# Hybrid decoder layer on one core: key weights in the values' region, the second norm's sums in PSUM, chunk 0's weight sums ahead of the FFN

## The chip, the core and the metric

The kernel runs on one core of a Trainium2 chip. Engines, as the profile names them: PE (matmul, with PEld for its weight loads), DVE (vector), ACT (scalar, activation), POOL (general), SP (issues most of the DMAs). Each has its own queue and runs it in order; semaphores tie them together. SBUF is the working memory (128 partitions), PSUM holds matmul outputs in eight banks of 128 x 512 fp32. The metric is device time in microseconds. The kernel before takes 1085.76 us, the median of three runs (1084.98 to 1085.92).

## The reference

One decoder layer over 1024 tokens of width 1024, fp32:

```python
h = rms_norm(x, mix_norm)
z = h @ w_in          # gq, gk, gv, gr, glr, sq, sk, sv
# gated linear attention (4 heads), sliding-window attention with sinks (8 query, 2 kv heads)
x = x + concat([o_gla, o_swa]) @ w_out
h2 = rms_norm(x, ffn_norm)
u = causal_dwconv(h2 @ w_up, conv_w, conv_b)      # 2 x 2816 columns, 3 taps
a, bval = split(u, 2)
return x + (silu(a) * bval) @ w_down
```

## The kernel before

**Numbers and tiles.** Every fp32 operand of a large matmul is split into a high part (a cast to fp32r) and a low part (source minus high part), and each product takes three passes: high x high, high x low, low x high (`PASSES`). `split` (L85) does this: ACT casts the high part, POOL (or the engine given) subtracts. Tokens lie in 8 tiles of 128. `big` holds the split, transposed activations of all tiles, first of the first norm, then of the attention output, then of the second norm.

**Stages.** One matmul stage follows another, each with a unit per token tile: query (`unit_q`), key with gate columns (`unit_k`, 272 columns), values (`unit_v`), gated q and k (`unit_g`), output gate (`unit_r`), and output projection in two halves of 512 columns (`unit_o`). The small matmuls of the two attentions run between them. The weights of a stage come as 4 raw loads (two row blocks each) into a ring of three raw tiles, and become 8 split pieces (`load_piece` L265, `piece` L256). The pieces lie in nine slots of 4 KB, w0 to w8, dealt out by the tuple `SLOTS` (L72): query 0 to 7, key 8 and 0 to 6, values 7, 8, 0 to 5, and so on. Key pieces fill only 272 of a slot's 512 columns.

**Key and value stage.** `kvl_post` (L325) takes a key tile out of PSUM: squares on ACT, sum on DVE, the power -1/2 on POOL (`rms_scale` L151, the power at L155), the scaled keys kn on DVE (L332). `kvl_tr` (L338) transposes kn on PE. The first norm's buffers (`px`) give way to the values' result `vg` (16 KB, `open_vg`), which the value units write.

**Second norm.** After the second half of a token tile's output projection, `norm2_stat` (L178) squares the row on ACT and takes the power on POOL; `norm2_tr` (L185) scales the row on DVE (L188, two halves) and transposes it on PE into two PSUM banks. Tiles 0 to 3 are split straight into `big`. For tiles 4 to 7, `norm2_sums` (L201) also forms the sums that the FFN's fast products need: b12 is copied by ACT from PSUM; T1 = b12 - b11 on POOL (on DVE for tile 7, `T1_DVE`); T3 = b22 - b12, T2 = b22 - T1, T4 = b21 - T2 on DVE, into four SBUF tiles; each is split into `big` or `ex`, the low parts partly on POOL, partly on DVE. The temporaries lie in the pool `pn`, whose space the FFN's pool `ff` takes over at `open_ff`.

**FFN.** The up projection is cut into 22 chunks of 128 columns of a and of b. A chunk is a 2 x 2 block product over halves of the width and halves of the tokens, done as seven products (`PROD`, L724) of 12 matmuls of 128x512: P1 (A11, B11), P2 (A12, B21), P3 (S4, B22), P4 (A22, T4), P5 (S1, T1), P6 (S2, T2), P7 (S3, T3). The weight sums are S1 = A21 + A22, S3 = A11 - A21, S2 = S1 - A11, S4 = A12 - S2, formed by POOL in place in the raw tiles; `up_operand` (L691) forms and splits them. Chunk 0 runs P1, P2, P3, P5, P6, P7, P4. Its P1 and P2 and chunk 1's come first (the list `LOW`), for they need token tiles 0 to 3 alone. From then on two chunks' products and the down projection (also by seven products, `down_pair`) interleave to the end.

**Order.** Each step is entered by hand with a due time (`at`, in units of a token tile; `at_us`, in us from the FFN's start TU), and the steps are emitted in order of that time. The framework then lays out each engine's order by a simulated timeline (`schedule_with_timeline_sim=True`), with the emitted order as priority: what is ready in the simulation may go ahead of what is not. A tile in a reused slot or in a reopened region waits for the last user of what lay there. PSUM banks are dealt alternately from two pools of four (`bank` L55); at the FFN's start all eight become fixed banks fb0 to fb3 and gb0 to gb3.

The due times that matter here, before:

```python
at(u + (1.9 if t < 7 else 1.3), norm2_tr, t)
if t >= 4:
    at(u + (SUMS if t < 7 else 1.33), norm2_sums, t)
...
at(TV - 0.9 + d, load_piece, "v", CV, 512, i, (None, None), dve)
...
for (ch, op), us in (((0, "A11"), EA), ((0, "A12"), EB), ((1, "A11"), -4), ((1, "A12"), -3.5),
                     ((0, "S2"), 1.74), ((0, "S4"), 1.75), ((0, "S1"), 1.77), ((0, "S3"), 1.9),
                     ((0, "A22"), 1.91)):
    at_us(us, up_operand, ch, op)
```

Of the kernel before, what the change touches and what calls it, by code (L numbers as in the profile page):

```python
# [34 lines left out]
def hymba_layer_kernel(ctx, tc, x, mix_norm, w_in, w_alpha2, b_alpha, gla_norm,  # L35
# [33 lines left out]
    w_late = {}  # L69
    swp = ExitStack()  # L70
    idp = swp.enter_context(tc.tile_pool(name="idp", bufs=1, side="right"))
    SLOTS = tuple(i % 9 for i in range(48)) + (9, 3, 4, 5, 6, 7, 8, 0)  # L72
    used = [0]

    def slot_tile(slot, name, dt=F32R):
# [106 lines left out]
        act.activation(h, acc, AF.Square, accum_out=ss)  # L182
        fin["r", t] = rms_scale(ss, D, 1, f"n2{t}", pn, "n2")

    def norm2_tr(t):  # L185
        h, acc, r = fin["h", t], fin["acc"][t], fin["r", t]
        for c in halves:
            dve.scalar_tensor_tensor(h[:, c], acc[:, c], r[:, 0:1], fin["ffn"][:, c],  # L188
                                     op0=ALU.mult, op1=ALU.mult)
        if t < 4:  # L190
            norm_tr(t, h, "n2")
            return
        pbs = fin["pb", t] = []
        for q in range(2):
            pt = bank(f"n2pt_{t}_{q}")
            for k in range(4):
                c = (q * 4 + k) * P
                pe.transpose(pt[:, k * P:(k + 1) * P], h[:, c:c + P], ident)
            pbs.append(pt.rearrange("p (k c) -> p k c", k=4))

    def norm2_sums(t):  # L201
        i, ex, pn, pbs = t - 4, fin["ex"], fin["pn"], fin["pb", t]

        def tmp(n):
            return pn.tile([P, 4, P], F32, tag=n, name=f"{n}_{t}", bufs=1)

        def put(src, dst, eng=None):
            split(src, dst[:, :, 0, :], dst[:, :, 1, :], eng)
# [4 lines left out]
        act.copy(b12, pbs[0])
        eng.tensor_sub(t1, b12, b11[:, :, 0, :])
# [3 lines left out]
        dve.tensor_sub(t3, pbs[1], b12)
# [463 lines left out]
    def load_chunk(ch):  # L682
        load_side(ch, 0)
        load_side(ch, 1)

    U_SLOT = {(0, "A11"): 1, (0, "A12"): 2, (1, "A11"): 3, (1, "A12"): 4, (0, "S2"): 6, (0, "S4"): 7,
              (0, "S1"): 8, (0, "S3"): 1, (0, "A22"): 2, (1, "S2"): 3, (1, "S1"): 1, (1, "S3"): 2,
              (1, "S4"): 3, (1, "A22"): 1}
    turn = [1]

    def up_operand(ch, name):  # L691
        ra, rb = raws["u", ch, 0], raws.get(("u", ch, 1), raws["u", ch, 0])
        a11, a12, a21, a22 = ra[:, 0:4], ra[:, 4:8], rb[:, 0:4], rb[:, 4:8]
        src = {"A11": a11, "A12": a12, "A21": a21, "A22": a22, "S2": a11, "S3": a21, "S4": a11}.get(name)
        if name == "S2":
            if ch:
                s1 = fin["ff"].tile([P, 4, P], F32, tag="s", name=f"S1_{ch}", bufs=1)
            else:
                s1 = slot_tile(0, "S1_0", F32)[:, 0].rearrange("p (k n) -> p k n", k=4)
            psb["S1", ch] = s1  # L700
            pool.tensor_add(s1, a21, a22)
            pool.tensor_sub(a21, a11, a21)
            pool.tensor_sub(a11, s1, a11)
        elif name == "S1":
            src = psb["S1", ch]
        elif name == "S4":
            pool.tensor_sub(a11, a12, a11)
# [302 lines left out]
    for t in range(NT):  # L1010
# [161 lines left out]
```

## Time and profile before

| | |
|---|---|
| runs | 1084.98, 1085.76, 1085.92 us |
| profiled execution | 1085.34 us, its span 1083.4 us |
| PE busy | 1067.0 us (98%) |
| DVE, POOL, ACT busy | 786.0 (73%), 659.5 (61%), 494.4 (46%) |
| mean granted clock of PE | 0.995 |
| largest matmul groups | down products 215.9 us, output projection 93.2 us, each up product of chunks 1 to 21 about 63 us |

Stages by PE's rows: query to about 63 us, keys to 91, values between 93 and 166, gates and attention to 324, output projection to 420, FFN from 420.8, last rows of the down projection from 1063.

Lines of the timeline read: start, duration (both us), engine, line of the kernel, operation, tile written <- tiles read, shape, count, and in brackets the idle time before it and what ended it. Where a count is over 1 the duration is that of the whole run of instructions. Rows of the windows read: stretch, its length, then busy time and count of PE, PEld, DVE, ACT and POOL, the granted clock of PE as a share of full speed, the DMA share and GB/s. A matmul of 128x512 shows as 0.39 us, but a row of twelve takes 2.81 us, for they overlap.

### The profile page before, as it was taken

Reading aid. Unit: us, or ns where it says so; the run is one execution under the profiler, and the core shown is the slowest. Engines: PE = TensorE matmul, PEld = TensorE weight load, DVE = VectorE, ACT = ScalarE, POOL = GpSimd, SP = SyncE. Lnnn points to the kernel's source line nnn. Section 1 sums busy time; section 2 is a strip of 40 time slices with the busy share of each in tenths; the row PEclk is TensorE's granted clock in tenths of the full one; section 3 lists DMA queues with packets and bytes.
Section 4 is the critical chain, followed back from the end, with each engine's and each line's share of the span. In section 5 each row is a group of like instructions: output and inputs, shape, how many; then the busy total and the mean of one; then the engine's idle time right before and its main releaser. Section 6 shows DMA issues by size and latency. Waiting matters only on the chain.

```text
span 1083.4 us, 13893 instructions
## 1 busy us (share of the span) xinstructions
PE 1067.0 (98%) x4976; PEld 856.4 (79%) x4976; DVE 786.0 (73%) x1269; ACT 494.4 (46%) x998; POOL 659.5 (61%) x523
## 2 busy tenths in 40 slices
PE   7999999999999999899999999999999999999998
PEld 5897778777788887678888888888888888888886
DVE  6646546555222368798997979797989899797976
ACT  6336656546231245444444444444444444444441
POOL 4355224234552248876978777786868797877750
PEclk9999999999999999899999999999999999999999
DMA  6124113102017200212111111212111111112104
GB/s 226 40 72 134 33 31 97 31 10 67 12 28 245 59 1 8 70 40 71 46 59 59 58 59 40 78 40 77 35 54 49 46 52 59 59 55 63 40 19 155
DMA packets 67342, 67.13 MB, mean 62 GB/s; under 512 B 4616, under 2 KB 51913, under 8 KB 67274
## 3 DMA queue, kind: packets, MB, share of 16 engines
q1 hardware_dynamic: 63432, 61.53, 18.2%
q10 hardware_dynamic: 3842, 4.73, 1.8%
q8 instruction: 39, 0.64, 0.3%
q14 instruction: 29, 0.24, 0.1%
HBM read 57.33 MB, written 4.19 MB: 57 GB/s over the span
## 4 chain that ended last, share of the span: by engine, by line
PE 96%; POOL 2%; DVE 1%; DMA 0%; ACT 0%; issue 0%; SPq 0%; POOLq 0%; ACTq 0%
PE fb L751 38%; PE dn_P L932 18%; PE do L273 8%; PE dg L273 4%; PE dr L273 4%; PE dv L273 4%; PE dq L273 3%; PE dk L273 2%; PE gb L751 2%; PE pv L434 1%; PE ppt L422 1%; PE dq L632 1%; PE fb L959 1%; PE dl L959 1%; PE ga L522 1%; PE sc L390 1%
## 5 line engine op out<-in xcount | busy, mean ns | idle before, releaser
L932 PE MATMUL dn_P<-dw,dg 128*128 128x512 f32 x840 | 215.9, 393 | 0.0
L936 DVE TENSOR_TENSOR acc<-acc,dn_P 128x1024 f32<-128x1024 f32 x140 | 169.9, 1214 | 61.3 <-PE dn_P L932 61.1
L932 PEld LDWEIGHTS dn_P<-dw,dg 128*128 128x128 f32 x840 | 157.6, 188 | 37.3 <-ACT dg L87 0.3
L273 PE MATMUL do<-wow,big 128*128 128x512 f32 x384 | 93.2, 398 | 0.0
L90 POOL TENSOR_TENSOR dw<-dn,dw 128x512 fp32r<-128x512 f32 x50 | 69.9, 1398 | 25.9 <-PE dn_P L932 22.3
L273 PEld LDWEIGHTS do<-wow,big 128*128 128x128 f32 x384 | 71.1, 188 | 16.2
L803 ACT COPY ca<-fb 128x512 f32<-128x512 f32 x62 | 36.4, 586 | 73.6 <-PE fb L751 73.5
L411 POOL TENSOR_TENSOR pr<-pr,sm 128x1024 f32<-128x1024 f32 (+1 forms) x16 | 28.6, 1787 | 65.7 <-DVE sm L409 38.6
L751 PE MATMUL fb<-big,A11w 128*128 128x512 f32 x252 | 63.2, 396 | 0.0
L751 PE MATMUL fb<-big,S1w 128*128 128x512 f32 x252 | 63.2, 396 | 0.0
L751 PE MATMUL fb<-big,S4w 128*128 128x512 f32 x252 | 62.9, 397 | 0.2 <-ACT ca L803 0.2
L751 PE MATMUL fb<-ex,S2w 128*128 128x512 f32 x252 | 62.9, 397 | 0.0
L751 PE MATMUL fb<-big,A12w 128*128 128x512 f32 x252 | 62.8, 396 | 0.0
L758 DVE SCALAR_TENSOR_TENSOR ua<-fb,cc,ua 128x511 f32<-128x511 f32 x84 | 62.2, 740 | 0.8 <-ACT ua L763 0.5
L751 PE MATMUL fb<-ex,S3w 128*128 128x512 f32 x252 | 62.7, 397 | 0.0
L751 PE MATMUL fb<-ex,A22w 128*128 128x512 f32 x252 | 62.5, 397 | 0.0
L751 PEld LDWEIGHTS fb<-big,S4w 128*128 128x128 f32 x252 | 47.3, 188 | 12.1 <-ACT ca L803 0.6
L751 PEld LDWEIGHTS fb<-big,A11w 128*128 128x128 f32 x252 | 47.4, 188 | 11.6
L751 PEld LDWEIGHTS fb<-big,S1w 128*128 128x128 f32 x252 | 47.4, 188 | 11.6
L751 PEld LDWEIGHTS fb<-ex,S2w 128*128 128x128 f32 x252 | 47.2, 188 | 11.6 <-ACT S2w L87 0.2
L751 PEld LDWEIGHTS fb<-ex,A22w 128*128 128x128 f32 x252 | 47.4, 188 | 11.4
L751 PEld LDWEIGHTS fb<-ex,S3w 128*128 128x128 f32 x252 | 47.4, 188 | 11.4
(425 smaller groups left out, 2475.3 us busy)
## 6 DMA issues: line engine op xcount, KB each, us to landing
up<-in_w_up_dram SPq DMA_DIRECT2D x44, 512.0 KB, 3.8
dn<-in_w_down_dram SPq DMA_DIRECT2D x22, 512.0 KB, 3.5
acc<-in_x_dram SPq DMA_DIRECT2D x8, 512.0 KB, 6.4
out_dram<-acc SPq DMA_DIRECT2D x16, 256.0 KB, 2.0
xt<-in_x_dram SPq DMA_DIRECT2D x7, 512.0 KB, 4.0
qraw<-in_w_in_dram SPq DMA_DIRECT2D x4, 512.0 KB, 7.4
vraw<-in_w_in_dram SPq DMA_DIRECT2D x4, 512.0 KB, 4.5
qt<-qt ACTq DMA_DIRECT2D x16, 128.0 KB, 2.2
```

Of the source, the lines that this page charges most:

```text
L90: (eng or pool).tensor_sub(lo, src, hi.bitcast(F32))
L273: pe.matmul(pb[:, :n], lhsT=big[:, t, k, ra, :], rhs=ws[k][:, rb, :n], start=(k == 0 and i == 0), stop=(k == KD - 1 and i == 2))
L390: pe.matmul(pbs[-1][:, j % 2, :], lhsT=q[:, g, qc], rhs=kt[:, g, kc], start=True, stop=False)
L411: pool.tensor_tensor(pr[:, :, s0:], pr[:, :, s0:], den[:, hs].rearrange("p (j o) -> p j o", o=1).broadcast_to((P, 4, n)), ALU.mult)
L422: pe.transpose(pb[:, j * P:(j + 1) * P], pr[:, j, b * P:(b + 1) * P], ident)
L434: pe.matmul(pb[g * 64:(g + 1) * 64, :], lhsT=vv[:, t - 1 + b, g * 64:(g + 1) * 64], rhs=pts[t, g][:, b, :], start=(b == b0), stop=(b == 1))
L751: pe.matmul(pb, lhsT=w[:, ra, k, :], rhs=b_operand(bn, k, rb), start=(onto is None and i == 0), stop=(i == 11), skip_group_check=onto is n ...
L758: dve.scalar_tensor_tensor(dst, src, w, dst, op0=ALU.mult, op1=ALU.add)
L803: act.copy(dst, pb)
L932: pe.matmul(pb[:, i], lhsT=g[:, ra, c:c + P], rhs=w[:, rb, :], start=(onto is None and n == 0), stop=(n == 2), skip_group_check=onto is no ...
L936: dve.tensor_add(acc, acc, pb)
L959: pe.matmul(pb, lhsT=g[:, ra, (t % 4) * P:(t % 4 + 1) * P], rhs=w[:, rb, :], start=(ch == NCH - 2 and i == 0), stop=(ch == NCH - 1 and i = ...
```

## The change

1. **Key pieces.** A new pool `kp`, opened when the first norm's buffers close and closed when `vg` opens, holds seven key pieces of [2, 272]; the eighth takes slot 6. `SLOTS` is dealt anew, so that queries take slots 7, 8, 0 to 5 and the later stages the same slots as before. The four value loads, with their splits, are due from 0.4 after the key stage's start on, 1.2 apart, not just ahead of the value stage.
2. **Second norm.** The scaling of the rows becomes a step of its own (`norm2_rows`), due right after the statistics. The sums are formed in the two PSUM banks themselves, all by DVE, and all low parts are DVE's; POOL has no part in them, and the four SBUF temporaries go. T2 is formed as T3 + b11. Tile 7's transposes and sums are due at 0.28 and 0.29 us, between the third and the fourth of the early products, not after them. Three tiles' banks are pinned to one of the two pools.
3. **FFN.** Chunk 0's four weight sums are formed at -12 us (`first_sums`), S1 in a tile of `pn` and S4 in A12's place; the splits then come in the order S4, S1, S2. S1 and S4 change slots. Chunk 1's A11 and A12 are split at -13 and -12.5 us, not at -4 and -3.5, into tiles of `pn` and not into slots 3 and 4.

```diff
+        for start, which in (("n2pt_6", "b"), ("do1_7", "a"), ("n2pt_3", "a")):
+            if name.startswith(start):
+                return ps[which].tile([P, 512], F32, tag="b", name=name)
...
-    SLOTS = tuple(i % 9 for i in range(48)) + (9, 3, 4, 5, 6, 7, 8, 0)
+    SLOTS = tuple((i + 7) % 9 for i in range(41)) + (9, 3, 4, 5, 6, 7, 8, 0)
...
     def norm2_sums(t):
...
-        b12, t1, t2, t3, t4 = (tmp(n) for n in ("b12", "t1", "t2", "t3", "t4"))
+        b12 = pn.tile([P, 4, P], F32, tag="b12", name=f"b12_{t}", bufs=1)
         b11, b21 = big[:, i, 0:4].bitcast(F32), big[:, i, 4:8].bitcast(F32)
-        eng = dve if t == T1_DVE else pool
-        act.copy(b12, pbs[0])
-        eng.tensor_sub(t1, b12, b11[:, :, 0, :])
-        eng.tensor_sub(t1, t1, b11[:, :, 1, :])
-        put(t1, big[:, t, 0:4])
-        put(pbs[1], big[:, t, 4:8], dve)
-        dve.tensor_sub(t3, pbs[1], b12)
-        dve.tensor_sub(t2, pbs[1], t1)
-        dve.tensor_sub(t4, b21[:, :, 0, :], t2)
-        dve.tensor_add(t4, t4, b21[:, :, 1, :])
-        put(t3, ex[:, 1, i], dve)
-        put(t2, ex[:, 0, i])
-        put(t4, ex[:, 2, i], dve)
+        act.copy(b12, p0)
+        put(p1, big[:, t, 4:8])
+        dve.tensor_sub(p0, p0, b11[:, :, 0, :])
+        dve.tensor_sub(p0, p0, b11[:, :, 1, :])
+        put(p0, big[:, t, 0:4])
+        dve.tensor_sub(p1, p1, b12)
+        put(p1, ex[:, 1, i])
+        dve.tensor_add(p1, p1, b11[:, :, 0, :])
+        dve.tensor_add(p1, p1, b11[:, :, 1, :])
+        put(p1, ex[:, 0, i])
+        dve.tensor_sub(p0, b21[:, :, 0, :], p1)
+        dve.tensor_add(p0, p0, b21[:, :, 1, :])
+        put(p0, ex[:, 2, i])
...
+            if name == "k" and k < 7:
+                w = fin["kw"][:, k]
+            else:
+                w = w_tile(f"{name}w{k}")
...
+    def open_kw():
+        sx.close()
+        fin["kp"] = ExitStack()
+        pk = fin["kp"].enter_context(tc.tile_pool(name="pkw", bufs=1, side="right"))
+        fin["kw"] = pk.tile([P, 7, 2, 272], F32R, name="kw")
...
+        fin["s1"] = pn.tile([P, 4, P], F32, name="s1_0")
...
+    def sums(s1, a11, a21, a22):
+        pool.tensor_add(s1, a21, a22)
+        pool.tensor_sub(a21, a11, a21)
+        pool.tensor_sub(a11, s1, a11)
+
+    def first_sums():
+        ra, rb = raws["u", 0, 0], raws["u", 0, 1]
+        s1 = psb["S1", 0] = fin["s1"]
+        sums(s1, ra[:, 0:4], rb[:, 0:4], rb[:, 4:8])
+        pool.tensor_sub(ra[:, 4:8], ra[:, 4:8], ra[:, 0:4])
...
-        at(u + (1.9 if t < 7 else 1.3), norm2_tr, t)
-        if t >= 4:
-            at(u + (SUMS if t < 7 else 1.33), norm2_sums, t)
+        at(u + 0.005, norm2_rows, t)
+        if t < 7:
+            at(u + 1.9, norm2_tr, t)
+        if 4 <= t < 7:
+            at(u + SUMS, norm2_sums, t)
...
-        at(TV - 0.9 + d, load_piece, "v", CV, 512, i, (None, None), dve)
+        at(TK + 0.4 + 1.2 * i, load_piece, "v", CV, 512, i, (None, None), dve)
...
-    at(7.3, open_vg)
+    at(7.05, open_kw)
+    at(TV - 0.05, open_vg)
...
-    for (ch, op), us in (((0, "A11"), EA), ((0, "A12"), EB), ((1, "A11"), -4), ((1, "A12"), -3.5),
-                         ((0, "S2"), 1.74), ((0, "S4"), 1.75), ((0, "S1"), 1.77), ((0, "S3"), 1.9),
+    for (ch, op), us in (((0, "A11"), EA), ((0, "A12"), EB), ((1, "A11"), -13), ((1, "A12"), -12.5),
+                         ((0, "S4"), 1.74), ((0, "S1"), 1.75), ((0, "S2"), 1.77), ((0, "S3"), 1.9),
                          ((0, "A22"), 1.91)):
         at_us(us, up_operand, ch, op)
+    at_us(-12, first_sums)
+    at_us(0.28, norm2_tr, 7)
+    at_us(0.29, norm2_sums, 7)
```

More of the change, by code (lines that the diff above doesn't have):

```diff
@@ L28 @@
 NPAIR = NCH // 2 - 1
-T1_DVE, SUMS, EA, EB = 7, 2.01, -25, -14
+SUMS, EA, EB = 2.01, -25, -14
 PASSES = ((0, 0), (0, 1), (1, 0))
@@ L183, in norm2_stat, with norm2_rows @@
         fin["r", t] = rms_scale(ss, D, 1, f"n2{t}", pn, "n2")
-    def norm2_tr(t):
+    def norm2_rows(t):
         h, acc, r = fin["h", t], fin["acc"][t], fin["r", t]
@@ L189, in norm2_tr @@
                                      op0=ALU.mult, op1=ALU.mult)
+    def norm2_tr(t):
+        h = fin["h", t]
         if t < 4:
@@ L201, in norm2_sums, with put @@
     def norm2_sums(t):
[L202 to L208, printed above, removed]
-        b12, t1, t2, t3, t4 = (tmp(n) for n in ("b12", "t1", "t2", "t3", "t4"))
-        b11, b21 = big[:, i, 0:4].bitcast(F32), big[:, i, 4:8].bitcast(F32)
-        eng = dve if t == T1_DVE else pool
-        act.copy(b12, pbs[0])
-        eng.tensor_sub(t1, b12, b11[:, :, 0, :])
-        eng.tensor_sub(t1, t1, b11[:, :, 1, :])
-        put(t1, big[:, t, 0:4])
-        put(pbs[1], big[:, t, 4:8], dve)
-        dve.tensor_sub(t3, pbs[1], b12)
-        dve.tensor_sub(t2, pbs[1], t1)
-        dve.tensor_sub(t4, b21[:, :, 0, :], t2)
-        dve.tensor_add(t4, t4, b21[:, :, 1, :])
-        put(t3, ex[:, 1, i], dve)
-        put(t2, ex[:, 0, i])
-        put(t4, ex[:, 2, i], dve)
+        i, ex, pn = t - 4, fin["ex"], fin["pn"]
+        p0, p1 = fin["pb", t]
+        def put(src, dst):
+            split(src, dst[:, :, 0, :], dst[:, :, 1, :], dve)
+        b12 = pn.tile([P, 4, P], F32, tag="b12", name=f"b12_{t}", bufs=1)
+        b11, b21 = big[:, i, 0:4].bitcast(F32), big[:, i, 4:8].bitcast(F32)
+        act.copy(b12, p0)
[11 more added lines that the diff above has]
+        put(p0, ex[:, 2, i])
     def norm_tr(t, h, tag):
@@ L260, in piece @@
             k = k2 * 2 + a
-            w = w_tile(f"{name}w{k}")
+            if name == "k" and k < 7:
+                w = fin["kw"][:, k]
+            else:
+                w = w_tile(f"{name}w{k}")
             split(rv[:, a, :], w[:, 0, :n], w[:, 1, :n], engs[a], hi_eng)
@@ L567, in hymba_layer_kernel @@
     gtiles = {}
+    def open_kw():
[3 more added lines that the diff above has]
+        fin["kw"] = pk.tile([P, 7, 2, 272], F32R, name="kw")
     def open_vg():
-        sx.close()
+        fin["kp"].close()
         pv = st.enter_context(tc.tile_pool(name="pvg", bufs=1, side="right"))
@@ L684, in load_chunk @@
         load_side(ch, 1)
-    U_SLOT = {(0, "A11"): 1, (0, "A12"): 2, (1, "A11"): 3, (1, "A12"): 4, (0, "S2"): 6, (0, "S4"): 7,
-              (0, "S1"): 8, (0, "S3"): 1, (0, "A22"): 2, (1, "S2"): 3, (1, "S1"): 1, (1, "S3"): 2,
+    U_SLOT = {(0, "A11"): 1, (0, "A12"): 2, (1, "A11"): -1, (1, "A12"): -2, (0, "S2"): 6, (0, "S4"): 8,
+              (0, "S1"): 7, (0, "S3"): 1, (0, "A22"): 2, (1, "S2"): 3, (1, "S1"): 1, (1, "S3"): 2,
               (1, "S4"): 3, (1, "A22"): 1}
     turn = [1]
+    def sums(s1, a11, a21, a22):
[7 more added lines that the diff above has]
+        pool.tensor_sub(ra[:, 4:8], ra[:, 4:8], ra[:, 0:4])
     def up_operand(ch, name):
@@ L693, in up_operand @@
         a11, a12, a21, a22 = ra[:, 0:4], ra[:, 4:8], rb[:, 0:4], rb[:, 4:8]
[L694 to L703, printed above, removed]
+        src = {"A11": a11, "A12": a12, "A21": a21, "A22": a22, "S2": a11, "S3": a21,
+               "S4": a11 if ch else a12}.get(name)
+        if name == "S2" and ch:
+            s1 = psb["S1", ch] = fin["ff"].tile([P, 4, P], F32, tag="s", name=f"S1_{ch}", bufs=1)
+            sums(s1, a11, a21, a22)
         elif name == "S1":
             src = psb["S1", ch]
-        elif name == "S4":
+        elif name == "S4" and ch:
             pool.tensor_sub(a11, a12, a11)
@@ L712, in up_operand @@
             U_SLOT[ch, name] = slot
-        w = slot_tile(slot, f"{name}w_{ch}").rearrange("p r (k n) -> p r k n", k=4)
+        w = fin["pn"].tile([P, 2, 512], F32R, name=f"{name}w_{ch}") if slot < 0 else slot_tile(slot, f"{name}w_{ch}")
+        w = w.rearrange("p r (k n) -> p r k n", k=4)
         split(src, w[:, 0], w[:, 1])
```

## Prediction

> **What bounds the kernel now.** I read the page first, then the waits of the matmul engine, then the granted clock around those waits.
>
> ```profile
> PE 1067.0 (98%) x4976; PEld 856.4 (79%) x4976; DVE 786.0 (73%) x1269; ACT 494.4 (46%) x998; POOL 659.5 (61%) x523
> PEclk9999999999999999899999999999999999999999
> ```
>
> PE is busy 98% of 1083.4 us and the change leaves every matmul in place, so only two things can move: the 16.4 us in which PE stands still, and the stretches in which its clock is low. The waits of PE name them (columns: total us, times, longest):
>
> ```profile
> PE gb L751 <- ACT S4w L87: 4.0, 1, 4.0
> ...
> PE kpt L341 <- DVE kn L332: 1.1, 1, 1.1
> ...
> PE fb L198 <- DVE n2h L188: 0.9, 1, 0.9
> PE gb L751 <- POOL S4w L90: 0.6, 1, 0.6
> PE n2pt L231 <- DVE n2h L188: 0.2, 1, 0.2
> ```
>
> The waits left out belong to the first 11 us, which no edit touches, but for one of 0.2 us later. So there are two places: the seam from keys to values (1.1 us), and the start of the FFN (4.0 + 0.9 + 0.6, with 0.2 just ahead). What follows each wait is in the windows (PE busy, PEld, DVE, ACT, POOL, then the granted clock):
>
> ```profile
> 102.00:103.00 1.00, 1.00 (x5) 0.83 (x4) 0.34 (x1) 0.95 (x3) 1.00 (x2) 0.82 0.60 137
> 103.00:104.00 1.00, 1.00 (x4) 0.73 (x3) 0.94 (x3) 0.71 (x2) 1.00 (x2) 0.50 0.49 127
> 104.00:105.00 1.00, 1.00 (x4) 0.81 (x3) 0.54 (x2) 0.00 (x0) 0.93 (x3) 0.50 1.02 158
> 105.00:106.00 1.00, 1.00 (x3) 0.76 (x3) 0.00 (x0) 0.57 (x2) 0.52 (x2) 0.50 0.92 332
> ...
> 432.00:446.00 14.00, 8.56 (x30) 6.24 (x29) 12.34 (x13) 5.62 (x10) 11.12 (x8) 0.76 0.38 114
> ...
> 439.50:440.50 1.00, 0.86 (x2) 0.77 (x3) 1.00 (x2) 0.29 (x1) 1.00 (x2) 0.50 0.00 0
> ...
> 443.50:444.50 1.00, 1.00 (x5) 0.76 (x5) 0.32 (x2) 0.62 (x1) 0.00 (x0) 0.76 0.00 0
> ```
>
> After each gap PE is full but slow. At the seam the clock takes 0.18 + 3 x 0.50 = 1.7 us; with the gap, **the seam costs 1.1 + 1.7 = 2.8 us**. At the FFN's start PE is busy 8.56 of 14.00 us, so 5.4 us stand still; half speed from the first S4 matmul to about 443.5 and 0.76 after takes some 0.4 + 0.5 x 3.9 + 0.24 = 2.6 us. **The FFN's start costs 8.0 us**, and with the 0.2 ahead of it the two places hold 11.0 us, 1.0% of the run. That is all that can be won.
>
> **Part 1: key pieces where the values will lie, values loaded early.** Why does kn come late at the seam? These are rows of the timeline (start, us, engine, line):
>
> ```profile
> 67.70 1.29 POOL L90 TENSOR_TENSOR vw<-vraw,vw 128x512 fp32r<-128x512 f32 x1
> ...
> 91.90 6.26 POOL L90 TENSOR_TENSOR vw<-vraw,vw 128x512 fp32r<-128x512 f32 x5
> 98.12 0.88 POOL L155 TENSOR_TENSOR k7r<-k7v,mhalf 128x2 f32<-128x2 f32 x1
> ```
> ```profile
> 68.00:91.00 23.00, 23.00 (x178) 21.94 (x178) 12.85 (x52) 9.68 (x33) 6.42 (x12) 1.00 0.22 62
> ```
>
> The last key tile's scale (k7r, L155) stands on POOL behind five value splits of 1.25 us. They come in a bunch because seven of the eight value weights go into slots that key weights hold until the last key matmuls. Only one value split ran early, at 67.70. With the keys in a tile of their own the values take the query's slots, all free when the key stage begins, and their due times are spread over it. From 68 to 91 us POOL is busy 6.4 of 23 us and DVE 12.9, so eight splits (8 x 1.3 = 10.3 us on POOL, eight short casts on DVE) fit. Two queues are passed: the four value loads move ahead on SP, where only key loads stand before them, and the splits move ahead of the small POOL powers of the key tiles. Such a power can now wait up to one split, 1.3 us, and PE then waits on that tile's transpose. Bounds of that: 0, as seven key tiles caused no PE wait before, to 1.1 + 1.7 = 2.8 if one gap like the old one appears. I take 0.3, near the lower end, because PE has other key units to run in between. Sum: **-2.8 + 0.3**.
>
> **Part 2: the FFN's start.** What PE does there, and what it waits for:
>
> ```profile
> 420.84 2.14 PE L751 MATMUL gb<-big,A11w 128*128 128x512 f32 x8
> ...
> 432.19 0.60 PE L198 MATMUL fb<-ident,n2h 128*128 128x128 f32 x4
> 433.70 0.63 PE L198 MATMUL fb<-ident,n2h 128*128 128x128 f32 x4 [0.91 <-DVE n2h L188]
> ...
> 523.83 2.81 PE fb L751 x12
> ```
> ```profile
> 429.06 0.99 POOL L155 TENSOR_TENSOR n27r<-n27v,mhalf 128x1 f32<-128x1 f32 x1
> ...
> 435.87 1.71 POOL L707 TENSOR_TENSOR up<-up 128x512 f32<-128x512 f32 x1
> 438.31 1.28 POOL L90 TENSOR_TENSOR S4w<-up,S4w 128x512 fp32r<-128x512 f32 x1 [0.73 <-ACT S4w L87]
> ...
> 421.00:432.00 11.00, 11.00 (x49) 8.82 (x49) 9.94 (x12) 5.46 (x11) 11.00 (x9) 1.00 0.00 0
> ```
>
> Four products that need no token tile above 3 run from 420.84 to 432.2. Then P3 wants S4w. POOL was full for the 11 us before (11.00 of 11.00) with chunk 0's four sums, its splits and the norm's own subtractions, and reached S4 (L707) last. The change puts the four sums (about 1.3 to 1.7 us each) before the last output tiles, when POOL has room (rows in part 3), splits S4 first, and takes the four POOL steps of each of the tiles 4 to 6 away. S4w's slot is free when the last output unit ends, just ahead of 420.84; one cast and one 1.3 us split later it is there, eight us before P3. The wait of 4.0 + 0.6 goes.
>
> **What is late next** is token tile 7, in its old form:
>
> ```profile
> 422.05 0.67 DVE L658 TENSOR_TENSOR acc<-acc,do 128x512 f32<-128x512 f32 x1
> 427.87 0.14 DVE L153 TENSOR_SCALAR n27v<-n2ss 128x1 f32<-128x1 f32 x1
> 430.09 3.47 DVE L188 SCALAR_TENSOR_TENSOR n2h<-acc,n27r,ffn 128x512 f32<-128x512 f32 x2 [0.44 <-POOL n27r L155]
> 434.67 1.78 DVE L214 TENSOR_TENSOR t<-b,big 128x512 f32<-128x512 f32 x1
> 436.98 0.68 DVE L218 TENSOR_TENSOR t<-fb,b 128x512 f32<-128x512 f32 x1
> ```
> ```profile
> 423.09 1.07 ACT L182 ACTIVATE n2h<-acc 128x1024 f32<-128x1024 f32 x1
> ...
> 432.88 0.59 ACT L213 COPY b<-fb 128x512 f32<-128x512 f32 x1
> 434.37 0.59 ACT L87 CAST big<-fb 128x512 fp32r<-128x512 f32 x1 [0.90 <-PE fb L198]
> ```
>
> Its scaled rows (L188) end at 433.6, after a stay of 3.7 us in DVE's queue behind other tiles' sums (the square ends at 424.2, n27v starts at 427.9), another on POOL. Three edits act here. The rows are due right after the statistics, both ahead of tile 6's sums. POOL is nearly empty, so rows take 1.4 us (the n20r row below) instead of 3.47. And the sums read PSUM: a DVE step with one operand there takes 0.68 beside a working POOL (L218), a step with both in SBUF 1.78 (L214). From the end of the last output unit at about 420: add 0.7, square 1.1, v 0.2, power 1.0 and up to one split of 1.3 ahead of it, rows 1.4 to 3.5: with 0.1 to 0.2 between steps ready between 425 and 428.4. The transposes now stand in PE's queue ahead of the fourth early product, that is, three products (3 x 2.81) after 420.84, at 429.3. They wait for nothing, with 0.9 us to spare at the worst.
>
> From their end (call it X, 430) the fourth product covers 2.8 us. ACT needs 0.6 for b12 and 0.6 for p1's cast: P3 can start at X + 1.3, at X + 2.5 if two other casts of 0.6 come first. DVE then issues 12 steps of 0.68, which overlap a little (0.6 apart), with ACT casts between: T1 at about X + 3.5, T3 X + 5.5, T2 X + 8, T4 X + 9. PE asks for them after P3, P5, P6, P7: T1 at X + 5.6, T2 at X + 8.4, T3 at X + 11.2, T4 at X + 14. T2 is the tight one, with 0.4 us. If P3 or T2 is late: nothing to 1 us each; I take 0.2 and 0.3. Sum: **-8.0 - 0.2 + 0.5**.
>
> **Part 3: does DVE hold it?** Each of tiles 4 to 6 gives DVE 12 sum steps instead of 7: 5 x 0.6 = 3.0 us more per round of 13 us.
>
> ```profile
> 389.00:402.00 13.00, 13.00 (x66) 10.42 (x65) 11.76 (x17) 6.02 (x12) 6.62 (x7) 1.00 0.00 0
> 402.00:415.00 13.00, 12.96 (x65) 10.39 (x64) 11.18 (x17) 6.54 (x13) 6.97 (x7) 1.00 0.00 1
> 415.00:421.00 6.00, 5.77 (x32) 4.58 (x31) 4.29 (x5) 3.75 (x7) 5.55 (x5) 1.00 0.00 0
> ```
> ```profile
> L90 DVE TENSOR_TENSOR ex<-t,ex 128x512 fp32r<-128x512 f32 x4 | 3.8, 956 | 0.0
> L188 DVE SCALAR_TENSOR_TENSOR n2h<-acc,n21r,ffn 128x512 f32<-128x512 f32 x2 | 2.4, 1261 | 0.7 <-POOL n21r L155 0.7
> ...
> L188 DVE SCALAR_TENSOR_TENSOR n2h<-acc,n20r,ffn 128x512 f32<-128x512 f32 x2 | 1.4, 747 | 0.7 <-POOL n20r L155 0.7
> ```
>
> Busy 11.8 and 11.2 of 13, it has 1.2 and 1.8 us free. But steps shrink: the rows by 1.0, the two ex splits of a round from 0.96 to 0.68 each. That leaves about 11.5 - 1.6 + 3.0 = 12.9 of 13: full. What slips is the sums, since rows and adds are due first; PE's transposes want only rows. The slip, 0 to 3 us by 415, is made up by 432: of the 17 us up to there DVE was busy 14.2, of which tile 7's rows alone lose 2 to contention that goes. POOL has 6 us free in each round for the moved sums and chunk 1's two early splits (6 x 1.3 = 7.8). Cost taken: 0.
>
> [...]
>
> **The sum.** -2.8 + 0.3 - 8.2 + 0.5 = -10.2. The profiled execution took 1085.34 us (span 1083.4 and 1.9 around it), 0.4 under the median of 1085.76. Forecast: span 1073.2, **1075.1 us**.
>
> **The rivals.**
>
> *Tile 7 stays late.* The compiler orders each engine by a simulated timeline, so the written times do not bind. If the rows still end at 433.6 while the transposes stand ahead of the fourth product, PE is blocked from 429.3 to about 433.7 with 2.8 us of ready work behind: 4.2 still and 2.6 of half speed, 6.8 instead of 8.0. Only 1.2 is won there: 1085.3 - 2.8 - 1.2 = **1081.3**. For it: DVE is full. Against: both queues that delayed it are relieved. 0.15.
>
> *The seam stays* or opens elsewhere in the key stage: 1075.1 + 2.8 = **1077.9**. For it: DVE is busy 12.9 of 23 us there and gets eight casts. 0.06.
>
> *The low clock at 102 us is not the gap's.* Then only the gap itself goes and 1.7 us stay: **1076.8**. For it: the fall comes 1.4 us after the gap. Against: the run's only other fall of this kind follows the other gap. 0.04. [...]
>
> *Nothing moves*: the scheduler puts sums and splits where they were. **1085.3**. 0.05.
>
> *VectorE becomes the bound of the second norm: slower.* If the 15 added steps of tiles 4 to 6 (9.0 us) find no room and the contention stays, tile 7's rows end at 433.6 + 9.0 = 442.6. PE, with the transposes ahead of the fourth product, stands from 429.3 to 442.6: 13.3 + 2.6 = 15.9 instead of 8.0, so 1085.3 + 7.9 - 2.8 = **1090.4**. It decides once the rows end after about 429.3 + (8.0 + 2.8 - 2.6) = 437.5. For it: 12.9 of 13. Against: rows go first, and the contention leaves with POOL's work. 0.10.
>
> **The numbers.** The forecast has 0.60. A difference under 0.2% (2.2 us) is no more than a measurement of this kernel can tell. The range from 1073.5 (all 11.0 won and a little more) to 1082 holds the forecast and the first three rivals, 0.85, less a few hundredths for their tails. Faster 0.85, within 0.2% 0.05, slower 0.10.
>
> **What would show it.** Right: PE waits on no S4w and no kn; the clock is whole from 60 to 1060 us; S4w's split lies before 425; tile 7's transposes stand between early products with no wait; T2's split ends within a few tenths of P6's need; POOL is nearly idle from 389 to 415 apart from the moved sums, and DVE nearly full. Wrong: a new wait of PE on n2h or on ex with a clock of 0.50 behind it, or key transposes waiting on POOL's powers from 70 to 90 us.

## The result, and the profile after

The kernel after takes 1076.78 us (median of 4 runs, 1076.08 to 1077.32) against 1085.53 (1084.98 to 1085.92) beside it: a ratio of 0.9919, interval 0.9902 to 0.9937. The profiled execution took 1077.32 us, its span 1075.5, that is 7.9 less than before. Two later executions, of 2523.76 and 4650.01 us, lie far from all others of their kernels, and the medians and ranges below leave them out. The forecast was 1075.1, and the two places it spoke of are indeed cleared. What it did not have are two new waits. PE's waits in the profile after (total us, times, longest):

```profile
PE n1pt L238 <- DVE n11v L158: 3.1, 1, 3.1
...
PE n2pt L238 <- DVE n2h L193: 2.2, 1, 2.2
PE gb L775 <- DVE gb L849: 1.2, 1, 1.2
```

No kn and no S4w is left. The first line belongs to the start, ahead of the first query matmul, which no edit touches; it was 2.1 us in the profile of before. PE's waits there add up to between 4.8 and 7.3 us over the fourteen profiles of this case (5.5 before, 6.4 after), so two profiles can differ by up to 2.5 us for that alone. Windows after (PE, PEld, DVE, ACT, POOL busy, then clock):

```profile
100.00:110.00 10.00, 10.00 (x51) 7.47 (x49) 4.37 (x15) 5.47 (x16) 0.95 (x4) 1.00 0.21 50
...
389.00:402.00 13.00, 13.00 (x66) 10.62 (x65) 11.89 (x22) 6.21 (x12) 1.10 (x2) 1.00 0.00 0
432.00:446.00 14.00, 14.00 (x61) 11.10 (x60) 11.33 (x18) 7.17 (x13) 11.02 (x9) 1.00 0.24 75
```

PE is full with a whole clock at the seam and at the FFN's start, where it was busy 8.56 of 14 us. DVE did not fill up in the rounds of tiles 4 to 6: 11.89 of 13.

The key stage on POOL (L95 is the split, L160 the power; lines as numbered after the change):

```profile
64.37 2.67 POOL L95 TENSOR_TENSOR vw<-vraw,vw 128x512 fp32r<-128x512 f32 x2 [0.36 <-DVE vw L94]
...
77.71 0.71 POOL L160 TENSOR_TENSOR k1r<-k1v,mhalf 128x2 f32<-128x2 f32 x1
...
97.87 0.69 POOL L160 TENSOR_TENSOR k7r<-k7v,mhalf 128x2 f32<-128x2 f32 x1
```

All eight value splits, the first two of them in the first row, end by 77.8. Powers of key tiles do stand behind them, as k1r does, but no transpose waits for one. Now the FFN's start (start, duration, engine, line):

```profile
421.01 1.29 POOL L95 TENSOR_TENSOR S4w<-up,S4w 128x512 fp32r<-128x512 f32 x1
...
426.48 1.40 DVE L193 SCALAR_TENSOR_TENSOR n2h<-acc,n27r,ffn 128x512 f32<-128x512 f32 x2
...
429.29 1.04 PE L206 MATMUL fb<-ident,n2h 128*128 128x128 f32 x8
...
432.93 2.97 PE L775 MATMUL gb<-big,S4w 128*128 128x512 f32 x12
...
438.56 2.14 PE L775 MATMUL gb<-ex,S2w 128*128 128x512 f32 x8
...
438.54 0.69 DVE L95 TENSOR_TENSOR ex<-fb,ex 128x512 fp32r<-128x512 f32 x1 [0.47 <-ACT ex L92]
...
448.43 3.06 PE L775 MATMUL gb<-ex,A22w 128*128 128x512 f32 x12 [1.20 <-DVE gb L849]
...
447.69 0.68 DVE L849 TENSOR_TENSOR gb<-ca,gb 128x512 f32<-128x512 f32 x1
```

S4w is split by 422.3. Tile 7's rows end at 427.9, its transposes run at 429.29 without a wait, and P3, P5 and P6 (432.93, then 438.56 for S2w) follow with no gap. T2's low part (438.54, ex) lands while P6 already works on the high parts. The last two rows are the second new wait: P4 of chunk 0 goes on in a bank that DVE reads for an addition (L849) right after P7. The first new wait lies 40 us earlier:

```profile
374.42 1.30 POOL L95 TENSOR_TENSOR A11w<-up,A11w 128x512 fp32r<-128x512 f32 x1 [0.98 <-ACT A11w L92]
375.68 1.29 POOL L95 TENSOR_TENSOR A12w<-up,A12w 128x512 fp32r<-128x512 f32 x1
376.93 1.29 POOL L710 TENSOR_TENSOR up<-up,up 128x512 f32<-128x512 f32 x1
378.18 0.56 POOL L160 TENSOR_TENSOR n20r<-n20v,mhalf 128x1 f32<-128x1 f32 x1
378.70 1.26 POOL L711 TENSOR_TENSOR up<-s,up 128x512 f32<-128x512 f32 x1
...
375.95 0.15 DVE L158 TENSOR_SCALAR n20v<-n2ss 128x1 f32<-128x1 f32 x1 [2.42 <-ACT n2h L187]
378.77 3.43 DVE L193 SCALAR_TENSOR_TENSOR n2h<-acc,n20r,ffn 128x512 f32<-128x512 f32 x2 [2.66 <-POOL n20r L160]
...
380.66 0.63 PE L238 MATMUL n2pt<-ident,n2h 128*128 128x128 f32 x4 [2.25 <-DVE n2h L193]
```

Tile 0's statistics are there at 376.1, but POOL is in a row of chunk 1's two splits and chunk 0's sums, so the power comes 2.1 us later; the next sums then run beside the scaled rows, which take 3.43 us (1.4 before). PE waits 2.25 us for them. In the kernel before POOL had next to nothing to do here (2.03 of 13 us, the fifth column), and the power started 0.15 us after the statistics:

```profile
376.00:389.00 13.00, 13.00 (x65) 10.54 (x64) 5.81 (x10) 4.68 (x9) 2.03 (x3) 1.00 0.00 0
```

### The profile page after: what moved, and what is told of

Its sections match the earlier page's. It is cut to its first block, busy times and chain, and to the rows that moved or that the text cites. A ratio compares the mean times of both kernels' runs of the same rounds, so it can differ in the third digit from the quotient of the medians.

```text
span 1075.5 us, 13899 instructions
## 1 busy us (share of the span) xinstructions
PE 1061.8 (99%) x4976; PEld 854.0 (79%) x4976; DVE 785.0 (73%) x1287; ACT 493.9 (46%) x998; POOL 635.6 (59%) x509
## 4 chain that ended last, share of the span: by engine, by line
PE 96%; DMA 1%; DVE 1%; ACT 1%; issue 0%; POOL 0%; SPq 0%; DVEq 0%; ACTq 0%
PE fb L775 38%; PE dn_P L956 18%; PE do L283 7%; PE dg L283 4%; PE dv L283 4%; PE dr L283 4%; PE dq L283 3%; PE dk L283 2%; PE pv L444 1%; PE ppt L432 1%; PE dq L649 1%; PE gb L775 1%; PE fb L983 1%; PE dl L983 1%; PE sc L400 1%; PE ga L532 1%
## 5 line engine op out<-in xcount | busy, mean ns | idle before, releaser
L95 POOL TENSOR_TENSOR dw<-dn,dw 128x512 fp32r<-128x512 f32 x50 | 69.9, 1398 | 27.4 <-PE dn_P L956 22.3
```

The costliest lines, as they stand in the source:

```text
L95: (eng or pool).tensor_sub(lo, src, hi.bitcast(F32))
```

## The experiments

Theory: the change is worth what the two places held, and pays a new wait because POOL's moved work comes in one bunch at tile 0's rows. Rivals: DVE is simply too full there; or tile 0's transposes are in the wrong place on PE and POOL has nothing to do with it. The first four kernels take the change apart.

**Part 1 alone, and the change without part 1.** The first kernel is before with these lines, the second after without them:

```diff
+    SLOTS = tuple((i + 7) % 9 for i in range(41)) + (9, 3, 4, 5, 6, 7, 8, 0)
+            if name == "k" and k < 7:
+                w = fin["kw"][:, k]
+        at(TK + 0.4 + 1.2 * i, load_piece, "v", CV, 512, i, (None, None), dve)
+    at(7.05, open_kw)
+    at(TV - 0.05, open_vg)
```

> The kernel before with the first part alone (key pieces in their own tile, value loads early). My theory: the seam goes with its low clock, 2.8 us less, about 1082.7; PE has no wait on kn, the clock stays 1.00 from 96 to 110 us, and the FFN's start still stands still 5.4 us. Rival, the low clock is not the gap's: 1.1 us less, 1084.4, with a fall of the clock near 102 us still there. Rival, the seam only moves: 1085.5.

> The changed kernel without the first part. My theory: the two places are independent, so the old seam comes back whole: 2.8 us more than the changed kernel, about 1079.6, with the kn wait of about 1.1 us and a clock of 0.50 behind it. Rival, the gap alone counts: 1077.9. Rival, the early keys and values did nothing and all came from the FFN's start: 1076.8.

Part 1 alone: 1083.18 us (1081.54 to 1084.1) against 1085.05, ratio 0.9981 (0.9972 to 0.9989), some 2 us. The wait on kn and the half clock behind it are gone, and the FFN's waits on S4w are the old ones:

```profile
100.00:104.00 4.00, 4.00 (x18) 2.54 (x17) 1.27 (x4) 2.60 (x8) 0.02 (x1) 1.00 0.35 81
```

The change without part 1: 1079.64 us (1078.62 to 1080.88), ratio 0.995 (0.9938 to 0.9963). The whole change did not run beside it. Its two series have the ratios 0.9919 and, below, 0.9937, so part 1 is worth 3.4 or 1.4 us on top of the rest (2.9 by the times as they stand). The profile has the seam back, as it was forecast, with half clock behind it:

```profile
PE kpt L348 <- DVE kn L339: 1.3, 1, 1.3
```

**Early weight sums alone; second norm alone.** Before with the early sums, chunk 1's A11 and A12 left in slots 3 and 4 at -4 and -3.5:

```diff
+    at_us(-12, first_sums)
+                         ((0, "S4"), 1.74), ((0, "S1"), 1.75), ((0, "S2"), 1.77), ((0, "S3"), 1.9),
```

And before with `norm2_rows`, the sums in PSUM by DVE, the pinned banks, and tile 7's new times:

```diff
+    at_us(0.28, norm2_tr, 7)
+    at_us(0.29, norm2_sums, 7)
```

> The kernel before with chunk 0's weight sums early and S4 split first (S1 in a tile of pn, S4 in slot 8), the norm as it was. My theory: PE no longer waits on S4w, but token tile 7 in its old form is next, late by DVE and POOL; 2 to 4 us are won at the FFN's start, and the new wait of about 2 us at tile 0's transposes (sums ahead of its power on POOL, near 378 us) is paid: 1083 to 1085.5. Rival, S4w alone was the cause: 7 to 8 us less at the FFN's start, about 1079.5.

> The kernel before with the second norm's part alone (sums in PSUM on DVE, rows early, tile 7 between the early products), weight sums as they were. My theory: POOL loses the norm's steps and reaches S4 some 4 us earlier, so S4w is waited for 0 to 2 us; the low clock may still come; tile 0's new wait of 2.2 us does not come, for POOL has no weight sums then: 1078 to 1081. Rival, S4w alone was the cause and it stays late by the sums: 1083 or more. Rival, VectorE overloaded: PE waits on n2h, over 1085.

Early sums alone: 1083.83 us (1082.93 to 1087.51), ratio 0.9993 (0.9984 to 1.0003). The S4w wait goes, and several of 0.3 to 1.4 us take its place, tile 7's first, with one of 3.3 us behind them (in the last section; the profiled execution took 1085.88 us, 2 over the median). So the first cause by the waits was worth next to nothing while the second stood close behind it. The wait of about 2 us that was expected at tile 0 came to 0.46, though the four sums are early here too: chunk 1's two splits stand later in this kernel. Second norm alone: 1081.52 us (1080.06 to 1083.12), ratio 0.9968 (0.9957 to 0.998), a little over what was expected. POOL still forms its sums late, so tile 7's rows are slow and S4w comes as late as 432.9:

```profile
428.33 3.48 DVE L192 SCALAR_TENSOR_TENSOR n2h<-acc,n27r,ffn 128x512 f32<-128x512 f32 x2 [0.18 <-POOL n27r L159]
...
431.22 1.73 POOL L94 TENSOR_TENSOR S4w<-up,S4w 128x512 fp32r<-128x512 f32 x1
```

Against 426.48 and 1.40 in the whole change: the two parts need each other. By the ratios the three parts alone win 2.1, 0.8 and 3.5 us, 6.3 of the 8.8 of the whole.

**Tile 0's transposes later.**

```diff
-            at(u + 1.9, norm2_tr, t)
+            at(u + (1.9 if t else 2.5), norm2_tr, t)
```

> The kernel after, with one edit: tile 0's transposes of the second norm stand behind the next whole output unit, not ahead of it. Theory (the new wait of 2.2 us at 378.4 is a wait for tile 0's scaled rows, which come late because POOL runs two splits and a sum ahead of the power n20r and two more sums beside the rows; PE had other ready work): the wait goes and nothing takes its place, 1076.8 - 2.2 = 1074.6 us, granted clock 1.00 on both sides. Rival (DVE and POOL are simply full there, so whatever stands next waits): the wait moves to tile 4's or tile 1's transposes, 1076.3 to 1077.

1074.88 us (1074.57 to 1075.79), ratio to before 0.9912 (0.9897 to 0.9927), its span 1072.8. The first series of the kernel after did not run beside it. Both kernels once more, side by side on another chip:

> The kernel after, once more, beside the next run on the same chip, and with a second profile: 1076.8 us if nothing depends on the chip. If the clock's fall after the 2.2 us gap at 378 comes in some executions and not in others, its windows from 380 to 385 may show 0.50 this time.

> The kernel after with tile 0's transposes behind the next output unit, once more, on the same chip as the kernel after: 1074.6 to 1074.9 us, 1.9 to 2.2 us below it, if that version beats the kernel after; no difference if the first comparison was one of chips.

1075.90 us (four runs from 1074.22 to 1076.37) against 1078.18 (1077.12 to 1079.04): 2.3 us less, and no run of the one reaches the other. Against before the two ratios are 0.9916 (0.9902 to 0.9929) and 0.9937 (0.9924 to 0.9951). In the first pair the times differ by 1.9 and the ratios by 0.8 us. The version with later transposes is thus the better one, but not by the gap alone: four of the five runs of the kernel after have a mean clock of 0.998, among them the profiled one with its fall here (last section), and against the fifth, 1077.12, the gain is 1.2. The second profile of that version shows why:

```profile
378.38 3.48 DVE L193 SCALAR_TENSOR_TENSOR n2h<-acc,n20r,ffn 128x512 f32<-128x512 f32 x2 [2.68 <-POOL n20r L160]
...
374.61 9.27 PE L283 MATMUL do<-wow,big 128*128 128x512 f32 x39
383.72 1.04 PE L238 MATMUL n2pt<-ident,n2h 128*128 128x128 f32 x8
```

The rows are as late and as slow as ever; PE has a unit of the projection to do meanwhile. Of the rival, 0.6 to 0.7 us is left as a wait on tile 4's rows. That DVE was simply too full is excluded: it stood idle for 2.68 us, waiting for POOL's power.

**Chunk 1's two splits away from POOL, and away from tile 0.** These ask whether POOL's queue is the cause. The kernel after, once with the splits on DVE:

```diff
+        split(src, w[:, 0], w[:, 1], dve if ch == 1 and name in ("A11", "A12") else None)
```

And once with the old slots and times, in which they can't run before the last output tiles:

```diff
-    U_SLOT = {(0, "A11"): 1, (0, "A12"): 2, (1, "A11"): -1, (1, "A12"): -2, (0, "S2"): 6, (0, "S4"): 8,
+    U_SLOT = {(0, "A11"): 1, (0, "A12"): 2, (1, "A11"): 3, (1, "A12"): 4, (0, "S2"): 6, (0, "S4"): 8,
-    for (ch, op), us in (((0, "A11"), EA), ((0, "A12"), EB), ((1, "A11"), -13), ((1, "A12"), -12.5),
+    for (ch, op), us in (((0, "A11"), EA), ((0, "A12"), EB), ((1, "A11"), -4), ((1, "A12"), -3.5),
```

> The kernel after, with the low parts of chunk 1's A11 and A12 formed by DVE, not by POOL; tile 0's transposes keep their place on PE. Theory (POOL's two extra splits before the power n20r make tile 0's rows late): without these 2.5 us POOL ends its sums earlier, n20r comes at about 377.3 and the rows, with no sum beside them, take 1.4 to 1.5 us: ready at about 379.2 against 378.4 wanted, so the wait falls from 2.2 to 0.8 us or less: 1075.4 us. Rival (the rows' own place on DVE, or the place of the transposes on PE, sets the wait): 2.2 us stay, 1076.8 us.

1078.44 us (1076.72 to 1078.99), ratio 0.9939 (0.9926 to 0.9951): a miss, and no answer to the question. The splits stood on DVE ahead of the addition that tile 0's statistics need, and beside POOL's sums:

```profile
374.79 1.78 DVE L95 TENSOR_TENSOR A12w<-up,A12w 128x512 fp32r<-128x512 f32 x1
376.49 0.68 DVE L675 TENSOR_TENSOR acc<-acc,do 128x512 f32<-128x512 f32 x1
...
378.44 0.15 DVE L158 TENSOR_SCALAR n20v<-n2ss 128x1 f32<-128x1 f32 x1 [1.28 <-ACT n2h L187]
```

The statistics came 2.5 us later (375.95 in the kernel after), and with rows of 1.42 us the wait was still 2.4. (The same condition went into the down projection's splits, where it never holds: they stay on POOL.)

> The kernel after, with chunk 1's A11 and A12 back in slots 3 and 4 and at their old due times, so that their splits can't run before the last output unit; tile 0's transposes keep their place on PE. Theory (POOL's two extra splits ahead of the power n20r make tile 0's rows late): POOL's four sums then run from 372 to 377.3, n20r follows at about 377.3, and the rows take 1.4 us without a sum beside them: ready at about 379.4 against 378.4 wanted, so the wait falls from 2.2 to about 1.0 us, and the time to 1075.6 us. Rival (the place of the transposes alone decides, whatever POOL does): 2.2 us stay, 1076.8 us.

Here the question is answered, though the time is not the expected one: 1079.95 us (1079.18 to 1081.24), ratio 0.9958 (0.9946 to 0.9971).

```profile
377.29 0.56 POOL L160 TENSOR_TENSOR n20r<-n20v,mhalf 128x1 f32<-128x1 f32 x1
...
377.88 1.42 DVE L193 SCALAR_TENSOR_TENSOR n2h<-acc,n20r,ffn 128x512 f32<-128x512 f32 x2 [3.18 <-POOL n20r L160]
...
378.78 0.63 PE L238 MATMUL n2pt<-ident,n2h 128*128 128x128 f32 x4 [0.66 <-DVE n2h L193]
...
420.15 0.63 PE L238 MATMUL n2pt<-ident,n2h 128*128 128x128 f32 x4 [1.05 <-DVE n2h L193]
...
438.93 3.04 PE L775 MATMUL gb<-big,S1w 128*128 128x512 f32 x12 [1.69 <-DVE ex L95]
```

Without the two splits the power is there at 377.9, the rows take 1.42 us, and tile 0's wait falls from 2.25 to 0.66 with the transposes in their old place. So POOL's bunch was the cause: the two splits of 1.6 us, the four sums of what is left. But the splits then run from 413.5 to 416 with three others behind them, tile 3's rows wait in turn (0.65 and 1.05), and P5 waits 1.69. In this profile the clock falls too (0.86 from 421 to 432): the first eight early matmuls take 3.66 us, against 2.14 in the kernel after. The work that makes a row late only moved to another row.

**Tile 7's transposes behind the early products.**

```diff
-    at_us(0.28, norm2_tr, 7)
-    at_us(0.29, norm2_sums, 7)
+    at_us(1.56, norm2_tr, 7)
+    at_us(1.716, norm2_sums, 7)
```

> The kernel after, with tile 7's transposes and sums put back behind the four early products. Theory (the fourth product is the cover that hides tile 7's split and sums): the transposes start 2.8 us later, at about 432.1, with no work behind them. P3 waits 1.3 us or so for ACT's two casts, and P6 about 2 us for T2, which needs some 9 us from the transposes' end and is asked for after 6.9: 3.3 us of stand, and 0 to 2 us of low clock if the fall comes, so 1076.8 + 3.3 = 1080.1 us, up to 1082. Rival (the relief of POOL and DVE alone was enough, the place of the transposes is worth nothing): 1076.8 us.

1079.35 us (1078.76 to 1080.51), ratio 0.9953 (0.994 to 0.9965): between 1.2 and 2.6 us over the two series of the kernel after, where 3.3 were expected. The place of the transposes is worth something, so the rival is out, but less than the theory said.

```profile
433.30 1.03 PE L206 MATMUL fb<-ident,n2h 128*128 128x128 f32 x8
435.12 3.08 PE L775 MATMUL gb<-big,S4w 128*128 128x512 f32 x12 [0.78 <-ACT big L92]
...
444.97 2.60 PE L775 MATMUL fb<-ex,S2w 128*128 128x512 f32 x10 [0.30 <-POOL S2w L95]
```

P3 waits 0.78 for ACT's cast, as it did not when the fourth product stood in between. P6 did not wait for T2, so that half of the expectation was too high: T2 was split 7.3 us after the transposes, not 9 (8.9 in the kernel after, where tile 6's last sums still stood in DVE's queue). The 0.30 in the last row is chunk 1's S2w.

**Sums in SBUF.** The kernel before with the second norm's part, its sums still all on DVE, but in SBUF tiles.

```diff
+        q1 = p1
+        p0, p1 = (pn.tile([P, 4, P], F32, tag=n, name=f"{n}_{t}", bufs=1) for n in ("t1", "t2"))
-        dve.tensor_sub(p0, p0, b11[:, :, 0, :])
+        dve.tensor_sub(p0, b12, b11[:, :, 0, :])
-        dve.tensor_sub(p1, p1, b12)
+        dve.tensor_sub(p1, q1, b12)
```

> The kernel before with the second norm's part of the change alone, but the sums T1 to T4 formed in SBUF tiles, all still by DVE. Theory (steps with an operand in PSUM run beside a working POOL at 0.68 us, steps with both operands in SBUF do not): where POOL is full, from 421 us on, some ten steps of tile 7 rise from 0.68 to between 1.2 and 1.8 us, T2 comes 4 to 8 us later than with PSUM, of which P6 and P7 of chunk 0 see 3 us or more: 1081.5 + 3 to 8 = 1084.5 to 1089.5 us. Rival (only the place and the order of the steps count): 1081.5 to 1082.0 us, as with the sums in PSUM.

1086.65 us (1083.46 to 1088.04), ratio 1.0013 (1.0004 to 1.0022), against 0.9968 with the sums in PSUM. By the ratios 4.9 us are the price of the place of the sums. The profiled execution is the fastest of the ten, so it shows less than that:

```profile
427.76 3.43 DVE L192 SCALAR_TENSOR_TENSOR n2h<-acc,n27r,ffn 128x512 f32<-128x512 f32 x2
431.11 1.76 DVE L230 TENSOR_TENSOR t<-big,t 128x512 f32<-128x512 f32 x1
...
429.66 0.68 PE L205 MATMUL fb<-ident,n2h 128*128 128x128 f32 x4 [2.05 <-DVE n2h L192]
```

Four steps with both operands in SBUF take 1.76 to 1.78 us beside POOL's steps, one 1.24, and those after 434, with POOL done, 0.67 to 0.69. The steps that lengthen were tile 6's, not tile 7's as expected: tile 7's rows stand behind them, end at 431.2, and PE waits for those, 2.05 and then 0.99 us. The clock falls behind these waits (0.82 from 432 to 446): the fourth early product takes 5.25 us, where a row of twelve takes 2.81.

**Both waits.** After, with tile 0's transposes later and, for the wait of 1.2 us, another product between chunk 0's P7 and P4.

```diff
-              (0, "S1"): 7, (0, "S3"): 1, (0, "A22"): 2, (1, "S2"): 3, (1, "S1"): 1, (1, "S3"): 2,
+              (0, "S1"): 7, (0, "S3"): 1, (0, "A22"): 2, (1, "S2"): 3, (1, "S1"): 7, (1, "S3"): 2,
-            at(u + 1.9, norm2_tr, t)
+            at(u + (1.9 if t else 2.5), norm2_tr, t)
-            at_us(prods[n - 2][2] + 0.01, up_operand, ch, PROD[name][0])
+            at_us(prods[n - 2][2] + 0.01 if (ch, name) != (1, "P5") else prods[n - 3][2] + 0.02, up_operand, ch, PROD[name][0])
```

> The kernel after, with tile 0's transposes behind the next output unit and, in the FFN, chunk 1's S1 in slot 7 (free after chunk 0's P5) and split one product earlier, so that chunk 1's P5 stands between chunk 0's P7 and P4. Theory (the 1.2 us at 447.2 is a lack of other ready work while DVE adds P7 and P5 in the bank that P4 goes on to use): both waits go, 1076.8 - 2.2 - 1.2 = 1073.4 us. Rival (the second wait only moves to the next product of the same chain): 1074.6 us.

1077.22 us (1075.3 to 1077.76), ratio 0.9925 (0.9913 to 0.9937): by the median 2.3 worse than later transposes alone on the same chip, but two of the five runs, 1075.30 and 1075.37, lie within that kernel's range. The wait at P4 is gone, but chunk 1's S3w comes late (0.59) and the first down product waits 0.81:

```profile
455.09 2.76 DVE L815 TENSOR_TENSOR ub<-ua,ub 128x2 f32<-128x2 f32 x1
...
460.05 3.03 PE L956 MATMUL dn_P<-dw,dg 128*128 128x512 f32 x12 [0.81 <-ACT dg L92]
```

Most of its loss in this profile stands at the start (a wait of 4.0 us on n11v, 2.0 in the other kernel), where nothing was edited. Why is open, so it isn't shown that the second edit itself loses anything.

## Why the prediction held, and where not

- **The seam** (-2.8 + 0.3): held. Alone it is worth 2 us, within the whole between 1.4 and 3.4. The 0.3 was not paid.
- **The clock behind a gap.** Shown as a cost that a gap brings at the seam, but not in every execution. The sum took 1.7 us as certain; in the run of the sums in SBUF a gap of 0.9 us in the same place had no fall (windows below), and three of the five runs of the change without part 1 have a mean clock of 1.000. The fall before starts at 102.64 by its rows, 2.0 us after the gap's end at 100.62, not 1.4.
- **The FFN's start** (-8.0 - 0.2 + 0.5): held, and the 0.5 was not paid. S4w, tile 7's rows, the transposes and T2 came where they were put, T2 with no margin. From the FFN's first matmul to the end the span fell by 662.6 - 654.7 = 7.9; -8.0 and +1.2 for the new wait make -6.8, and of the other 1.1 two small gaps of before (0.14 at 450.6 and 0.20 at 462.4) give 0.3.
- **"DVE 12.9 of 13"**: 11.89 and 11.73. The added steps were there, each about 0.69 us with its operand in PSUM. Contention that I left in the sum had gone with POOL's work (1.10 of 13 us, 6.62 before): in the round from 389 tile 1's rows took 1.41 us (2.44 before) and no split took 1.77 any more.
- **"POOL has 6 us free in each round ... Cost taken: 0"**: this is the step that failed. The room was counted over the rounds from 389 on, 13 us long, and 7.8 us of work were more than the 6 free there. But the work didn't go there. Due 13 and 12 us ahead of the FFN's start at 420.8, the two splits and three of the sums ran in one bunch from 374.4 to 381.6, some 30 us before that, in a stretch of which the prediction shows no row of POOL. POOL was busy there for 2.03 us of 13 before, so the average has room there too; what cost 2.25 us is that the bunch stands ahead of and beside tile 0's rows. The splits in their old slots show it (0.66 left), and so do the later transposes, with which the wait is gone.
- **The end of the chain of chunk 0's products** was not looked at: the sum stops at T2 and T4. P4's bank, read by DVE at L849 behind four convolution steps, cost 1.2 us.
- With these, and without the 0.3 and 0.5 that were not paid, -10.2 + 2.25 + 1.2 - 0.8 makes -7.6. The first query matmul comes 0.9 us later (11.99 against 11.06), which no edit touches: -6.6. With the two small gaps of before it is -7.0, against 7.9 measured. The other 0.9, most of it in the FFN, isn't placed. That the forecast is only 1.7 us off, with 3.45 us of new waits that it didn't have, is thus partly luck.
- That the rows are a step of their own was not taken back alone, so its share in tile 7's gain isn't shown.
- None of the rivals happened. *The low clock is not the gap's* named 1076.8, and 1076.78 was measured, but that is chance: the clock is whole from 100 to 110. *Tile 7 stays late* came closest in kind: a late row did block PE with the transposes ahead of ready work, but of tile 0, not 7.
- One sign that was named for being wrong did come, a new wait on n2h with a clock of 0.50 behind it: the wait in both profiles of the kernel after, the clock in the second.

## What to carry to other kernels

Room on an engine is worth looking at where the moved work will stand, not as an average over a round: list who waits behind it in its queue and who runs beside it. When a matmul queue waits for a step of another engine, try moving ready work ahead of the wait: here that won 1 to 2 us, and two tries to make the step early won nothing. And where two late inputs stand one behind the other, taking away the first alone shows next to nothing (1083.83 of 1085.05).

## What the runs showed of the hardware

**The clock.** The kernel after, profiled twice, has the same gap of 2.2 us at 378.4. In its first execution the clock stays whole; in the second it falls. First a row of the first, then rows of the second:

```profile
381.00:382.00 1.00, 1.00 (x7) 0.87 (x6) 1.00 (x1) 0.58 (x1) 0.65 (x1) 1.00 0.00 0
```
```profile
380.00:381.00 1.00, 0.26 (x2) 0.29 (x3) 1.00 (x2) 0.00 (x0) 0.92 (x2) 0.76 0.00 0
381.00:382.00 1.00, 1.00 (x5) 0.95 (x4) 1.00 (x1) 0.14 (x1) 0.72 (x1) 0.50 0.00 0
382.00:383.00 1.00, 1.00 (x4) 0.76 (x3) 1.00 (x3) 0.55 (x2) 0.00 (x0) 0.50 0.00 0
383.00:384.00 1.00, 1.00 (x4) 0.81 (x3) 0.46 (x1) 1.00 (x2) 0.00 (x0) 0.53 0.00 0
```

The seam likewise: first the kernel before, then the one with the sums in SBUF, whose wait on kn is 0.9 us:

```profile
102.00:106.00 4.00, 4.00 (x12) 3.14 (x11) 1.82 (x4) 2.23 (x6) 3.45 (x6) 0.58 0.76 188
```
```profile
102.00:106.00 4.00, 4.00 (x19) 3.22 (x18) 1.82 (x4) 2.32 (x7) 3.46 (x6) 1.00 0.75 182
```

At half clock, (0.24 + 0.50 + 0.50 + 0.47) / 0.50 = 3.4 us, and 4 x 0.42 / 0.50 = 3.4 us. Five other falls after a single gap, in the profiles of the early sums alone, the second norm alone, the change without part 1, tile 7's transposes behind and chunk 1's splits on DVE, sum to 3.4 us as well: each of these seven lasts 3.4 us and costs 1.7 where PE has work, whatever the gap, from 1.1 to 2.4 us. Such gaps brought it in some executions and not in others, and one of 3.3 us brought none (early sums alone, the clock 1.00 in every window from 460 to 474). What decides it isn't shown.

How often it falls shows in each run's mean clock, for 1.7 us of 1077 make 0.998 out of 1.000. The kernel after had 1.000 in its first four runs, and 0.998 in four of the next five: those took 1078.12 to 1079.04 us, the fifth 1077.12. With chunk 1's splits on DVE, three runs with 0.998 took 1078.44 to 1078.99 us, and two with 1.000 took 1076.72 and 1077.46.

**VectorE beside GpSimd.** In the kernel with the early sums alone a step of 128x2 elements took 4.89 us, where its kind takes 0.70 in the mean of 44 and the next one 0.15, with POOL's steps one after another beside it (first DVE, then POOL):

```profile
455.91 4.89 DVE L799 TENSOR_TENSOR ub<-ua,ub 128x2 f32<-128x2 f32 x1
...
461.69 0.15 DVE L799 TENSOR_TENSOR ub<-ua,ub 128x2 f32<-128x2 f32 x1
```
```profile
455.76 1.31 POOL L90 TENSOR_TENSOR S3w<-up,S3w 128x512 fp32r<-128x512 f32 x1
...
459.49 1.29 POOL L90 TENSOR_TENSOR A22w<-up,A22w 128x512 fp32r<-128x512 f32 x1
```

It ended with the fourth POOL step beside it, and PE waited 3.3 us at the end of that chain. The step of 2.76 us in the kernel with both waits is another: it ended with the third POOL step beside it. Of the steps of 128x512 elements in the run of the sums in SBUF, four with both operands in SBUF took 1.76 to 1.78 us beside POOL's steps, and the later ones 0.67 to 0.69 once POOL was done; one with an operand in PSUM took 0.68 beside a POOL step (L218 at 436.98 in the profile before). Why the two short steps lasted as long as four and three POOL steps isn't shown.
